# A two-block transformer on one core: gates' forget row after the second decay, 29 slabs split ahead, a later spread of the latents' norms, two merging products interleaved

## The chip, the core and the metric

One of the cores of a Trainium2 chip runs the whole program: TensorE (PE, matmuls), VectorE (DVE), ScalarE (ACT), GpSimd (POOL) and SyncE (SP), whose queue issues nearly all DMAs. The metric is the device time of one execution in microseconds. The kernel before takes 1064.96 us (median of three runs, 1063.67 to 1065.72).

## What is computed

One sequence of 512 tokens, width 1024, in fp32, through two blocks. The reference, cut to its lines of substance:

```python
# block 1: three mixers, then an MLP
h = rmsnorm(x, ln1); z = h @ w_in          # u_pool, gq, gk, gv, gg, ga, fq, fk, fv, ff
log_a = log_sigmoid(ga @ w_a_up + b_a) / 16        # GLA: per-channel decay, cumulated in chunks of 64
o = (q*exp(b-ref) . k*exp(ref-b), causal) v + (q*exp(b)) S_prev      # GLA output, per-head norm, silu gate
F = cumsum(log_sigmoid(ff + b_f))                  # FoX: forget row of 8 heads
p = softmax(q k^T / 8 + F_t - F_s)                 # FoX attention
x = x + concat(pool, gla, fox) @ w_o
x = x + (silu(gate) * up) @ w_down                 # gate, up = rmsnorm(x, ln2) @ w_gu, width 2816
x = rmsnorm(x, ln_f)
# block 2: MLA and DSA side by side
q_lat, c_kv, k_rope, z_a, q_b, k_b, v_b, z_b, q_idx, k_idx, w_idx, gate_a, gate_b = rmsnorm(x) @ w_in_2
q = rmsnorm(q_lat) @ w_uq; k, v = rmsnorm(c_kv) @ w_ukv; q_pe, k_pe = rope(...)
y_a = chunk-causal softmax attention (8 heads) * silu(z_a)
score = sum_h relu(q_idx . k_idx) * w_idx;  top-128 keys per query
y_b = softmax attention on those keys with a relative bias (8 heads) * silu(z_b)
merged = sigmoid(gate_a) * (y_a @ w_o_a) + sigmoid(gate_b) * (y_b @ w_o_b)
out = rmsnorm(x + merged @ w_out)
```

## The kernel before

**Products.** An fp32 operand is split into two parts that TensorE takes at full rate, hi (L188, an ACT copy) and lo (L190, source minus hi, on DVE or POOL). A product is three matmuls per 128-row slice: hi x hi, hi x lo, lo x hi (`dense`, L207; all matmuls are recorded at L151, transposes at L158). A slab of weights is 128 x 1024 (512 KB): `weight` (L196) loads it raw (`wr`) and splits it into `wh` and `wl`, and every third or so of the lo parts goes to POOL. For block 2, 33 slabs are split during block 1's MLP: `store` (L247) loads `sr`, ACT makes `sh`, POOL makes `sl`, and two DMAs write them to DRAM (`h_...`, `l_...`). `ready` (L237) later loads both parts back, or, for a slab that is not stored, calls `weight`.

**Order.** PE's order is written by hand: generators yield delays in ns of a modelled clock (`QKW`, `RSW`, `LATR` and the like), and a loop runs whichever is due, filling with products. The other engines' instructions are ordered by a scheduler, each engine then runs its own in order, and each waits for the semaphores of what it reads. SP issues its DMAs in order too, so a load that waits for its buffer holds up all behind it.

**The places touched.** (1) The GLA stage has two chains, f = 0 and 1 (`chain`, L753). `gates` (L608) makes the low-rank gate `ga` and the forget logits of FoX, and from these at once the forget row `F` (log-sigmoid L458 to L467 on 8 x 512, a scan at L620). `decay` (L655) makes a chain's log-sigmoid on 128 x 512 and its scan L660; `state` (L687) transposes the scaled keys (`kt`, copied by ACT at L693) and multiplies them with the values (`sc<-gv`); `output` (L715) makes the masked intra-chunk scores (`at`, L722) and multiplies them with the values (`pv<-at`). (2) `mlp` (L887) runs in two halves of 11 gate/up pairs (`w1gu`) and then 8 down products (`w1d`, slabs `wd` of 128 x 1408, hi and lo `wdh` and `wdl`). `relative` (L868) writes a 2.6 MB table (`shear`) in the first half's down products. The list `ahead` names the slabs to store; one is stored behind each gate/up pair but the first, one behind each down product of half 0, one behind each odd one of half 1. (3) `rstd` (L314) of the two latents of MLA: column sums, 1/sqrt, two parts (L298, L299), then after `RSW` = 800 ns of modelled clock the spread over 128 rows by eight matmuls with an identity (`tr<-identr,part`). (4) `merge_b` (L1312): eight output slices m, each a product of the DSA output (`lat`, four slices of 128) with `w2ob`; m = 0 and 1 share one slab. Before it `merge_a` products (L1246, closing at L1252) use the same three banks `mm`.

Of the kernel before, what the change touches and what calls it, by code (L numbers as in the profile page):

```python
# [20 lines left out]
P = 128  # L21
# [12 lines left out]
XR = 7  # L34
XO = 4
RSW = 800
RRW = 3300
KTW = 800
ATW = 2400
# [3 lines left out]
QKW = 500  # L43
# [41 lines left out]
class Body:  # L85
# [225 lines left out]
        self.spreaded = getattr(last, "ins", last)  # L311
        return r

    def rstd(self, sums, n):  # L314
        with self.tc.high_priority():
            c = self.inv_sqrt(self.col_sum(sums)[0], n)
            parts = self.parts(c)
        yield RSW
        with self.tc.high_priority():
            return self.spread(parts), c  # L320

# [261 lines left out]
    def gla_phase(self, ctx, h, R, Rc, mix, mp, b, fd, psg, held, V, proj):  # L583
        nc, A = self.nc, self.A
        gp = self.pool(ctx, "gla")
        new = b
# [21 lines left out]
        def gates():  # L608

            z, t = new()[:64], self.tmp()[:64]  # L610
            nc.scalar.activation(t, psg[64:], AF.Copy)
            with self.tc.issue_after(self.parted):
                nc.vector.tensor_tensor(z, psg[:64], t, op=OP.add)
            nc.vector.tensor_tensor(ga, z[:16], R[:16], op=OP.mult)
            f = new()[:8]
            nc.vector.tensor_tensor(f, z[32:40], R[32:40], op=OP.mult)
            F = self.log_sigmoid(f, self.gain("b_f", 0, 8), 8, new)
            one = new()[:8]
            nc.gpsimd.memset(one, 1.0)
            nc.vector.tensor_tensor_scan(F, one, F, 0.0, op0=OP.mult, op1=OP.add)  # L620
            nc.sync.dma_start(fd, F)

# [32 lines left out]
        def decay(f, q, k):  # L655
            ps = self.bank("tr")
            self.mm(ps, wau[:, f * P:(f + 1) * P], ga)
            la = self.log_sigmoid(ps, self.gain("b_a", f), P, new)
            bc = new()
            nc.vector.tensor_tensor_scan(bc, rmask, la, 0.0, op0=OP.mult, op1=OP.add)  # L660
            b3 = c3(bc)
            r = {}

            def scaled(name, base, src, scale):
                e = new()
                nc.scalar.activation(e, src, AF.Exp, scale=scale)
                nc.vector.tensor_tensor(e, base, e, op=OP.mult)
                r[name] = e

            def minus(c):  # L670
                d = new()
                nc.vector.tensor_tensor(c3(d), b3, b3[:, :, c:c + 1].to_broadcast([P, 8, 64]), op=OP.subtract)
                return d

            d = minus(63)
            scaled("kl", k, d, -1 / 16)
            dec = gp.tile([P, 8], F32, tag="dec", name="dec", bufs=2)
            nc.scalar.activation(dec, b3[:, :, 63], AF.Exp, scale=1 / 16)
            nc.vector.memset(dec[:, 0:1], 0.0)
            r["dec"] = dec  # L680
            d = minus(31)
            scaled("qi", q, d, 1 / 16)
            scaled("ki", k, d, -1 / 16)
            scaled("qx", q, bc, 1 / 16)
            return r
# [67 lines left out]
        def chain(f, held=None):  # L753
            if f == 0:
                gates()
            q, k = yield from qk(f, held)
            yield QKW + 3000 * (held is not None)
            r = decay(f, q, k)
            yield DECW
            sb = yield from state(f, r)  # L760
            gs[f] = yield from gate(f)
            yield GOW
            yield from output(f, r, sb, gs[f])

        gs = {}

        def pooling(f):

# [118 lines left out]
    def mlp(self, ctx):  # L887
        nc, A, x = self.nc, self.A, self.x
# [28 lines left out]
        t2 = lambda name, a, b: [("w2s", T2[name] + i, 1024) for i in range(a, b)]  # L917
        ahead = [("w2m", 0, KD * 72)] + t2("c_kv", 0, 2) + t2("q_idx", 0, 2) + t2("q_lat", 0, 3) + [("w2kv_v", 0, 1024)]
        ahead += t2("gate_b", 0, 8) + [("w2uq_r", 0, 768), ("w2pair", 0, 640)]
        for p in range(4):  # L920
            ahead += t2("gate_a", 2 * p, 2 * p + 2 if p < 3 else 6) + t2("z_a", p, p + 1)
            ahead += [("w2pair", p + 1, 640)] if p < 3 else []
        ahead = deque(ahead)
        relative = self.relative(wd)
        turns = []
        for half in range(2):
# [15 lines left out]
                    self.store(wd, *ahead.popleft())  # L942
            for m in range(KD):
                ps = self.all(self.dense(down(m, half), act, kt=FH))
                if (m % 2 or half == 0) and ahead:
                    self.store(wd, *ahead.popleft())
                if half == 0 and m < 2:
                    next(relative)
# [40 lines left out]
    def block2(self, ctx, psm, psc):  # L989
# [88 lines left out]
        def latent(name, n, gname, ps=None):  # L1078
# [10 lines left out]
                self.square_into(ss, z, j == 0)  # L1089
                out.append((zh, zl))  # L1090
            yield LATR
            r, c = yield from self.rstd([ss], n * P)
            return out, r, c

        V, V2 = [[], []], [[], []]
# [211 lines left out]
        gf = [at("qf", 1), at("kf", 1)]  # L1307
        for c in range(2):
            nc.sync.dma_start(gf[c], A["gf"][:, c * 512:(c + 1) * 512].to_broadcast([P, 512]))
        mg, wb, wo = [], {}, {}  # L1310

        def merge_b(m):  # L1312
            ga, gb = self.sx(), at("z", 3)
            nc.sync.dma_start(ga, kept["ma", m])
            nc.sync.dma_start(gb, kept["gate_b", m])
            if m % 2 == 0:
                wb[0] = self.weight(A["w2ob"][m // 2])
            ps = self.all(self.dense(wb[0], yb, kt=4, w0=(m % 2) * 512))
            nc.vector.scalar_tensor_tensor(gb, gb, 1.0, ps, op0=OP.add, op1=OP.mult)
            nc.vector.tensor_tensor(ga, ga, gb, op=OP.add)  # L1320
            hi = at("V", 8, dt=F32R)
            lo = qk(F32R) if m < 6 else self.kst()
            self.split_scaled(hi, lo, ga, 0.5)
            mg.append((hi, lo))
# [205 lines left out]
```

## Time and profile before

| | |
|---|---|
| median of three runs | 1064.96 us |
| profiled execution | 1063.43 us, of which its span 1061.7 |
| PE busy | 1042.3 us, 98% of the span, 5264 matmuls |
| DVE, ACT, POOL busy | 644.2 (61%), 548.3 (52%), 371.1 (35%) |
| granted TensorE clock, mean | 0.996 of full speed |
| DMA | 177.38 MB, mean 167 GB/s |

The profile page gives these sums. What it does not give is where PE stands still: that is in the view of waits of PE, and in tables of windows, which show the granted clock beside the busy time of each engine.

### The profile page before, as it was taken

The numbers are of one execution on the slowest core, as the hardware profiler recorded it, in microseconds if no ns is written. First come the engines' busy times: TensorE is split into PE (matmuls) and PEld (weight loads), VectorE is DVE, ScalarE is ACT, GpSimd is POOL, SyncE is SP. The second block draws the span as 40 slices with busy tenths as digits, with TensorE's granted clock in tenths as the row PEclk, the third lists the DMA queues.
The fourth block names the chain that finished last, engine by engine and source line by source line (L and its number), as shares of the span: only waits on it lengthen the run. The fifth ranks groups of instructions, "written<-read, shape, count | busy, mean of one in ns | idle before, by whom it ended". The sixth has DMA issues, their size and how long they took to land.

```text
span 1061.7 us, 14307 instructions
## 1 busy us (share of the span) xinstructions
PE 1042.3 (98%) x5264; PEld 864.3 (81%) x5264; DVE 644.2 (61%) x1141; ACT 548.3 (52%) x956; POOL 371.1 (35%) x213
## 2 busy tenths in 40 slices
PE   9999999999999999999999999999999999999997
PEld 6788977788888877888888888888888898888786
DVE  7754488866554523445433435799995556787652
ACT  7763478746343322333325545645555657777233
POOL 1233331233464531445424410010003345655354
PEclk9999999999999999999999999999999999999999
DMA  6312122126667688876777244464553323435842
GB/s 228 105 60 80 41 100 90 59 78 219 217 229 252 231 276 312 291 241 206 242 260 254 97 139 159 154 219 160 178 183 120 111 78 120 129 99 162 279 146 80
DMA packets 60126, 177.38 MB, mean 167 GB/s; under 512 B 7000, under 2 KB 11496, under 8 KB 60056
## 3 DMA queue, kind: packets, MB, share of 16 engines
q1 hardware_dynamic: 56968, 170.15, 47.6%
q10 hardware_dynamic: 2448, 4.22, 1.0%
q0 software_dynamic: 640, 2.10, 0.5%
q8 instruction: 42, 0.69, 0.3%
q14 instruction: 28, 0.23, 0.1%
HBM read 134.66 MB, written 44.40 MB: 169 GB/s over the span
## 4 chain that ended last, share of the span: by engine, by line
PE 47%; DVE 10%; DMA 3%; ACT 2%; issue 1%; SPq 1%; POOL 1%; ACTq 0%; DVEq 0%; POOLq 0%
PE mm L151 39%; PE sc L151 3%; DVE score L1068 2%; PE pv L151 2%; PE tr L158 2%; DVE m L1067 2%; DMA wd<-in_w1d 2%; PE tr L151 1%; DVE kst L190 1%; SPq L251 1%; DVE s L400 1%; DVE z L1203 1%; DMA z<-gate_a 1%; DVE pl L418 1%; DVE score L1052 1%
## 5 line engine op out<-in xcount | busy, mean ns | idle before, releaser
L151 PE MATMUL mm<-hh,wh 128*128 128x512 f32 (+2 forms) x808 | 323.2, 400 | 0.1
L151 PE MATMUL mm<-hl,wh 128*128 128x512 f32 (+3 forms) x808 | 315.2, 390 | 0.6 <-DVE hl L526 0.5
L151 PE MATMUL mm<-hh,wl 128*128 128x512 f32 (+1 forms) x800 | 312.4, 391 | 0.0
L190 POOL TENSOR_TENSOR wl<-wr,wh 128x1024 fp32r<-128x1024 f32 x74 | 186.6, 2522 | 328.6 <-ACT wh L188 307.2
L188 ACT ACTIVATE wh<-wr 128x1024 fp32r<-128x1024 f32 (+1 forms) x110 | 115.1, 1046 | 175.3 <-PE mm L151 150.1
L151 PEld LDWEIGHTS mm<-hh,wh 128*128 128x128 f32 (+1 forms) x808 | 152.3, 189 | 30.8 <-issue 1.3
L151 PEld LDWEIGHTS mm<-hh,wl 128*128 128x128 f32 (+1 forms) x800 | 150.1, 188 | 32.1
L151 PEld LDWEIGHTS mm<-hl,wh 128*128 128x128 f32 (+2 forms) x808 | 151.8, 188 | 29.1 <-DVE hl L526 1.8
L190 POOL TENSOR_TENSOR sl<-sr,sh 128x1024 fp32r<-128x1024 f32 (+3 forms) x32 | 81.9, 2558 | 81.0 <-DMA l_w2s<-sl 52.0
L151 PE MATMUL mm<-fh,wdh 128*128 128x512 f32 x176 | 71.0, 404 | 1.6 <-ACT wdh L188 1.6
L151 PE MATMUL mm<-fh,wdl 128*128 128x512 f32 x176 | 70.3, 400 | 0.9 <-DVE wdl L190 0.9
L151 PE MATMUL mm<-fl,wdh 128*128 128x512 f32 x176 | 70.1, 398 | 0.0
L938 DVE TENSOR_TENSOR u<-mm,R 128x512 f32<-128x512 f32 x22 | 15.2, 691 | 67.2 <-PE mm L151 67.2
L418 DVE TENSOR_TENSOR pl<-tr,ph 128x128 fp32r<-128x128 f32 (+1 forms) x96 | 45.9, 483 | 13.2 <-ACT ph L417 12.2
L402 ACT ACTIVATE s<-s,m 128x128 f32<-128x128 f32 (+1 forms) x64 | 35.8, 560 | 32.0 <-DVE m L400 31.6
L190 DVE TENSOR_TENSOR fl<-u,fh 128x512 fp32r<-128x512 f32 x22 | 42.4, 1925 | 14.7 <-ACT fh L188 14.7
L188 ACT ACTIVATE sh<-sr 128x1024 fp32r<-128x1024 f32 (+3 forms) x32 | 31.7, 990 | 37.3 <-DMA h_w2s<-sh 30.2
L949 DVE TENSOR_TENSOR x<-mm,x 128x512 f32<-128x512 f32 x16 | 11.1, 691 | 65.0 <-PE mm L151 65.0
L190 DVE TENSOR_TENSOR wl<-wr,wh 128x1024 fp32r<-128x1024 f32 (+1 forms) x35 | 42.9, 1226 | 11.0 <-ACT wh L188 10.6
L329 POOL TENSOR_TENSOR ss<-ss,t 128x512 f32<-128x512 f32 x21 | 29.7, 1423 | 55.3 <-ACT t L328 43.5
L151 PE MATMUL mm<-wh,hh 128*128 128x256 f32 x160 | 46.6, 291 | 0.0
L417 ACT ACTIVATE ph<-tr 128x128 fp32r<-128x128 f32 (+1 forms) x96 | 40.4, 425 | 10.1 <-PE tr L158 9.4
(343 smaller groups left out, 2053.3 us busy)
## 6 DMA issues: line engine op xcount, KB each, us to landing
wr<-in_w1gu SPq DMA_DIRECT2D x44, 512.0 KB, 4.6
sr<-in_w2s SPq DMA_DIRECT2D x25, 512.0 KB, 5.0
h_w2s<-sh SPq DMA_DIRECT2D x25, 512.0 KB, 2.9
l_w2s<-sl SPq DMA_DIRECT2D x25, 512.0 KB, 3.4
wh<-h_w2s SPq DMA_DIRECT2D x25, 512.0 KB, 3.7
wl<-l_w2s SPq DMA_DIRECT2D x25, 512.0 KB, 4.6
wd<-in_w1d SPq DMA_DIRECT2D x16, 704.0 KB, 5.7
wr<-in_w1s SPq DMA_DIRECT2D x15, 512.0 KB, 3.5
```

The lines of the kernel that those rows point to most:

```text
L151: self.nc.tensor.matmul(out, l, r, start=start, stop=stop)
L158: self.nc.tensor.transpose(out, src, self.ident if ident is None else ident)
L188: last = self.nc.scalar.activation(hi, src, AF.Copy)
L190: (eng or self.nc.vector).tensor_tensor(lo, src, hi.bitcast(F32), op=OP.subtract)
L329: return (eng or nc.gpsimd).tensor_tensor(ssum, ssum, sq, op=OP.add)
L402: nc.scalar.activation(s[:, :n], s[:, :n], AF.Exp, scale=-1.0, bias=m[:, 0:1], accum_out=m[:, 1:2])
L417: nc.scalar.activation(hi, trv, AF.Copy)
L418: nc.vector.tensor_tensor(lo, trv, hi.bitcast(F32), op=OP.subtract)
L938: nc.vector.tensor_tensor(u, ps, self.R2, op=OP.mult)
L949: nc.vector.tensor_tensor(x[m], ps, x[m], op=OP.add)
L1067: nc.vector.max(out=m8, in_=s)
L1068: nc.vector.match_replace(s, m8, s, -3.4e38)
```

## The change

- `gates` only keeps the logits `f`; the log-sigmoid and scan of the forget row are a function `forget`, called inside the second decay, behind its product with `wau`. The chain f = 0 takes its decay after `QKW` + 1000 instead of + 3000 ns.
- The list `ahead` loses four slabs (pairs' slab 3, `z_a` 3, `gate_a` 4 and 5), and in half 0 of the MLP a slab is stored only behind odd down products. The four slabs are loaded raw and split where they are used.
- The latents' `rstd` waits `LSW` = 3000 instead of `RSW` = 800 ns before the spread.
- The first two products of `merge_b` are written by `first_two`: two banks, slices k = 0 to 2 of both, then k = 3 of both.

```diff
--- before.py
+++ after.py
@@ -34,6 +34,7 @@
 XR = 7
 XO = 4
 RSW = 800
+LSW = 3000
 RRW = 3300
 KTW = 800
 ATW = 2400
@@ -311,11 +312,11 @@
         self.spreaded = getattr(last, "ins", last)
         return r
 
-    def rstd(self, sums, n):
+    def rstd(self, sums, n, lag=RSW):
         with self.tc.high_priority():
             c = self.inv_sqrt(self.col_sum(sums)[0], n)
             parts = self.parts(c)
-        yield RSW
+        yield lag
         with self.tc.high_priority():
             return self.spread(parts), c
 
@@ -612,8 +613,11 @@
             with self.tc.issue_after(self.parted):
                 nc.vector.tensor_tensor(z, psg[:64], t, op=OP.add)
             nc.vector.tensor_tensor(ga, z[:16], R[:16], op=OP.mult)
-            f = new()[:8]
+            logits["f"] = f = new()[:8]
             nc.vector.tensor_tensor(f, z[32:40], R[32:40], op=OP.mult)
+
+        def forget():
+            f = logits["f"]
             F = self.log_sigmoid(f, self.gain("b_f", 0, 8), 8, new)
             one = new()[:8]
             nc.gpsimd.memset(one, 1.0)
@@ -655,6 +659,8 @@
         def decay(f, q, k):
             ps = self.bank("tr")
             self.mm(ps, wau[:, f * P:(f + 1) * P], ga)
+            if f == 1:
+                forget()
             la = self.log_sigmoid(ps, self.gain("b_a", f), P, new)
             bc = new()
             nc.vector.tensor_tensor_scan(bc, rmask, la, 0.0, op0=OP.mult, op1=OP.add)
@@ -754,7 +760,7 @@
             if f == 0:
                 gates()
             q, k = yield from qk(f, held)
-            yield QKW + 3000 * (held is not None)
+            yield QKW + 1000 * (held is not None)
             r = decay(f, q, k)
             yield DECW
             sb = yield from state(f, r)
@@ -762,7 +768,7 @@
             yield GOW
             yield from output(f, r, sb, gs[f])
 
-        gs = {}
+        gs, logits = {}, {}
 
         def pooling(f):
 
@@ -918,8 +924,8 @@
         ahead = [("w2m", 0, KD * 72)] + t2("c_kv", 0, 2) + t2("q_idx", 0, 2) + t2("q_lat", 0, 3) + [("w2kv_v", 0, 1024)]
         ahead += t2("gate_b", 0, 8) + [("w2uq_r", 0, 768), ("w2pair", 0, 640)]
         for p in range(4):
-            ahead += t2("gate_a", 2 * p, 2 * p + 2 if p < 3 else 6) + t2("z_a", p, p + 1)
-            ahead += [("w2pair", p + 1, 640)] if p < 3 else []
+            ahead += t2("gate_a", 2 * p, 2 * p + 2 if p < 2 else 4) + t2("z_a", p, min(p + 1, 3))
+            ahead += [("w2pair", p + 1, 640)] if p < 2 else []
         ahead = deque(ahead)
         relative = self.relative(wd)
         turns = []
@@ -942,7 +948,7 @@
                     self.store(wd, *ahead.popleft())
             for m in range(KD):
                 ps = self.all(self.dense(down(m, half), act, kt=FH))
-                if (m % 2 or half == 0) and ahead:
+                if m % 2 and ahead:
                     self.store(wd, *ahead.popleft())
                 if half == 0 and m < 2:
                     next(relative)
@@ -1089,7 +1095,7 @@
                 self.square_into(ss, z, j == 0)
                 out.append((zh, zl))
             yield LATR
-            r, c = yield from self.rstd([ss], n * P)
+            r, c = yield from self.rstd([ss], n * P, LSW)
             return out, r, c
 
         V, V2 = [[], []], [[], []]
@@ -1307,15 +1313,33 @@
         gf = [at("qf", 1), at("kf", 1)]
         for c in range(2):
             nc.sync.dma_start(gf[c], A["gf"][:, c * 512:(c + 1) * 512].to_broadcast([P, 512]))
-        mg, wb, wo = [], {}, {}
+        mg, wb, wo, head = [], {}, {}, []
+
+        def first_two():
+
+            wb[0] = self.weight(A["w2ob"][0])
+            out = [self.bank("mm") for _ in range(2)]
+            for ks in (range(3), range(3, 4)):
+                for m in range(2):
+                    for k in ks:
+                        (hi, lo), (ah, al), c = wb[0], yb[k], slice(m * 512 + k * P, m * 512 + (k + 1) * P)
+                        self.mm(out[m], hi[:, c], ah, k == 0, False)
+                        self.mm(out[m], hi[:, c], al, False, False)
+                        self.mm(out[m], lo[:, c], ah, False, k == 3)
+            return out
 
         def merge_b(m):
             ga, gb = self.sx(), at("z", 3)
             nc.sync.dma_start(ga, kept["ma", m])
             nc.sync.dma_start(gb, kept["gate_b", m])
-            if m % 2 == 0:
-                wb[0] = self.weight(A["w2ob"][m // 2])
-            ps = self.all(self.dense(wb[0], yb, kt=4, w0=(m % 2) * 512))
+            if m < 2:
+                if m == 0:
+                    head.extend(first_two())
+                ps = head[m]
+            else:
+                if m % 2 == 0:
+                    wb[0] = self.weight(A["w2ob"][m // 2])
+                ps = self.all(self.dense(wb[0], yb, kt=4, w0=(m % 2) * 512))
             nc.vector.scalar_tensor_tensor(gb, gb, 1.0, ps, op0=OP.add, op1=OP.mult)
             nc.vector.tensor_tensor(ga, ga, gb, op=OP.add)
             hi = at("V", 8, dt=F32R)
```

The number of matmuls is the same, and so are the instructions of DVE, ACT and POOL in number and kind; SP issues 358 DMAs instead of 374. Lines below L311 have a number one or more higher after the change.

**ACT in the GLA stage**, from the scaling of chain 0's keys to the end of chain 1's log-sigmoid (`wh<-wr` is the hi part of a weight slab, `b<-tr` at L693 the copy of the transposed keys, L705 and L712 chain 0's state, L462 to L464 a log-sigmoid). Before:

```order
L666 ACTIVATE b<-b 128x512 x3
L188 ACTIVATE wh<-wr 128x1024 x2
L693 ACTIVATE b<-tr 128x512
L705 ACTIVATE b<-sc 64x256 x4
L712 ACTIVATE ph<-b 64x7x64 x2
L188 ACTIVATE wh<-wr 128x1024
L462 ACTIVATE b<-tr,gains 128x512
L463 ACTIVATE b<-b 128x512
L464 ACT_TABLE_LOAD
L464 ACTIVATE b<-b 128x512
```

After, from that copy (L699) on; two `wh<-wr` stand right ahead of the first row:

```order
L699 ACTIVATE b<-tr 128x512
L189 ACTIVATE wh<-wr 128x1024
L711 ACTIVATE b<-sc 64x256 x4
L463 ACTIVATE b<-b,gains 8x512
L718 ACTIVATE ph<-b 64x7x64 x2
L464 ACTIVATE b<-b 8x512
L465 ACT_TABLE_LOAD
L465 ACTIVATE b<-b 8x512
L189 ACTIVATE wh<-wr 128x1024
L463 ACTIVATE b<-tr,gains 128x512
L464 ACT_TABLE_LOAD
L464 ACTIVATE b<-b 128x512
```

The copy of the keys now stands ahead of the third slab instead of behind both; the forget row's log-sigmoid (8x512), which stood at the stage's start, now lies between chain 0's state and chain 1's log-sigmoid. That one ends two rows below the second fence (a table load and L465 on 128x512), so that three table loads stand there where one stood. On PE the four transposes of the keys and the eight `sc<-gv` products behind them stand nine 128x512 matmuls earlier, and chain 1's product with `wau` 18 128x256 matmuls earlier in its stage.

**SP in the down products of half 0**, from the shear table on (`sr` loads a slab to be stored, `h_` and `l_` write its parts, `wd` loads a down slab). Before:

```order
L884 DMA shear<-gd 1024x1x640
L251 DMA sr<-in_w2s 128x1024
L258 DMA h_w2s_3619<-sh 128x1024
L258 DMA l_w2s_3621<-sl 128x1024
L251 DMA sr<-in_w2s 128x1024
L900 DMA wd<-in_w1d 128x1408 x2
L258 DMA h_w2s_3670<-sh 128x1024
L258 DMA l_w2s_3672<-sl 128x1024
L251 DMA sr<-in_w2s 128x1024
L900 DMA wd<-in_w1d 128x1408
```

After:

```order
L890 DMA shear<-gd 1024x1x640
L252 DMA sr<-in_w2s 128x1024
L906 DMA wd<-in_w1d 128x1408
L259 DMA h_w2s_3742<-sh 128x1024
L906 DMA wd<-in_w1d 128x1408
L259 DMA l_w2s_3744<-sl 128x1024
L252 DMA sr<-in_w2s 128x1024
L906 DMA wd<-in_w1d 128x1408
L259 DMA h_w2s_3834<-sh 128x1024
L906 DMA wd<-in_w1d 128x1408
```

The first `wd` stood fifth behind the shear table and now stands second; between two `wd` there are now one or two of the stores' DMAs instead of three.

**PE in the first products of `merge_b`**; `lat` are the four slices of the DSA output, the one with the highest number the last to be made. Before (the end of the first product, the start of the second):

```order
L151 MATMUL mm_9244<-lat_8994,wh_9240 128x512
L151 MATMUL mm_9244<-lat_8995,wh_9240 128x512
L151 MATMUL mm_9244<-lat_8994,wl_9241 128x512
L151 MATMUL mm_9244<-lat_9207,wh_9240 128x512
L151 MATMUL mm_9244<-lat_9208,wh_9240 128x512
L151 MATMUL mm_9244<-lat_9207,wl_9241 128x512
L151 MATMUL mm_9267<-lat_8339,wh_9240 128x512
L151 MATMUL mm_9267<-lat_8340,wh_9240 128x512
L151 MATMUL mm_9267<-lat_8339,wl_9241 128x512
L151 MATMUL mm_9267<-lat_8676,wh_9240 128x512
L151 MATMUL mm_9267<-lat_8677,wh_9240 128x512
L151 MATMUL mm_9267<-lat_8676,wl_9241 128x512
```

After (the second bank's three slices, then the last slice in the first bank):

```order
L152 MATMUL mm_9213<-lat_8307,wh_9208 128x512
L152 MATMUL mm_9213<-lat_8308,wh_9208 128x512
L152 MATMUL mm_9213<-lat_8307,wl_9209 128x512
L152 MATMUL mm_9213<-lat_8644,wh_9208 128x512
L152 MATMUL mm_9213<-lat_8645,wh_9208 128x512
L152 MATMUL mm_9213<-lat_8644,wl_9209 128x512
L152 MATMUL mm_9213<-lat_8962,wh_9208 128x512
L152 MATMUL mm_9213<-lat_8963,wh_9208 128x512
L152 MATMUL mm_9213<-lat_8962,wl_9209 128x512
L152 MATMUL mm_9212<-lat_9175,wh_9208 128x512
L152 MATMUL mm_9212<-lat_9176,wh_9208 128x512
L152 MATMUL mm_9212<-lat_9175,wl_9209 128x512
```

Nine matmuls of the second product have moved ahead of the first one that reads the last slice.

## Rows read from the trace of the kernel before

**Rows 1.** Waits of PE: line, waited for, us in total, times, longest.
```profile
PE sc L151 <- ACT b L693: 1.8, 1, 1.8
PE mm L151 <- DVE lat L190: 1.6, 1, 1.6
PE mm L151 <- ACT wdh L188: 1.6, 1, 1.6
...
PE tr L151 <- DVE part L298: 1.1, 2, 0.9
PE mm L151 <- DVE wdl L190: 0.9, 1, 0.9
...
PE tr L151 <- DVE part L299: 0.5, 1, 0.5
```

**Rows 2.** Windows: length, busy PE, PEld, DVE, ACT, POOL, PEclk, DMA share, GB/s.
```profile
48.00:54.00 6.00, 6.00 (x29) 4.97 (x30) 1.81 (x2) 3.53 (x6) 0.00 (x0) 0.72 0.27 89
418.00:422.00 4.00, 4.00 (x12) 3.10 (x11) 2.52 (x1) 1.45 (x2) 2.37 (x1) 0.57 0.93 297
```

**Rows 3.** Timeline, GLA stage, ACT: start, duration, operation, [idle before, releaser].
```profile
29.18 1.28 ACT L464 ACT_TABLE_LOAD   x1
...
46.27 1.06 ACT L188 ACTIVATE wh<-wr 128x1024 fp32r<-128x1024 f32 x1 [3.87 <-DMA wr<-in_w1s]
47.23 0.58 ACT L693 ACTIVATE b<-tr 128x512 f32<-128x512 f32 x1
49.05 1.62 ACT L705 ACTIVATE b<-sc 64x256 f32<-64x256 f32 x4 [1.25 <-PE sc L151]
...
55.85 0.69 ACT L462 ACTIVATE b<-tr,gains 128x512 f32<-128x512 f32 x1 [0.61 <-PE tr L151]
...
58.52 0.63 ACT L464 ACTIVATE b<-b 128x512 f32<-128x512 f32 x1
```

**Rows 4.** Timeline, GLA stage, PE (two rows) and DVE (one).
```profile
47.86 1.72 PE L151 MATMUL sc<-gv,b 64*128 64x128 f32 x16 [1.83 <-ACT b L693]
...
71.33 1.58 PE L151 MATMUL pv<-at,gv 128*64 128x128 f32 x16
...
68.93 0.74 DVE L722 COPY_PREDICATED at<-c_gmask,sc 128x512 f32<-128x512 int32 x1
```

**Rows 5.** Timeline, down products of half 0: SP's queue, ACT, DVE; a window.
```profile
388.40 6.83 SPq L251 DMA_DIRECT2D sr<-in_w2s  x1
...
397.83 3.92 SPq L900 DMA_DIRECT2D wd<-in_w1d  x2
...
414.14 1.38 ACT L188 ACTIVATE wdh<-wd 128x1408 fp32r<-128x1408 f32 x1 [3.13 <-DMA wd<-in_w1d]
...
415.55 1.62 DVE L190 TENSOR_TENSOR wdl<-wd,wdh 128x1408 fp32r<-128x1408 f32 x1 [8.57 <-ACT wdh L188]
...
396.00:400.00 4.00, 4.00 (x18) 3.21 (x18) 0.92 (x2) 1.39 (x1) 0.00 (x0) 1.00 0.89 294
```

**Rows 6.** Latents and MLA: DVE's rope splits, then two windows as in rows 2.
```profile
667.10 2.08 DVE L190 TENSOR_TENSOR qk<-y,qk 32x512 fp32r<-32x512 f32 x2 [0.42 <-ACT qk L188]
...
680.00:700.00 20.00, 20.00 (x90) 16.47 (x89) 17.22 (x29) 11.54 (x21) 4.78 (x3) 1.00 0.59 203
740.00:760.00 20.00, 20.00 (x104) 16.93 (x103) 19.70 (x55) 11.43 (x25) 1.47 (x1) 1.00 0.58 197
```

**Rows 7.** Timeline: a DVE split in MLA; then the merge, DVE, POOL, PE.
```profile
791.51 0.68 DVE L190 TENSOR_TENSOR ya<-y,ya 128x512 fp32r<-128x512 f32 x1
...
988.17 2.08 DVE L190 TENSOR_TENSOR lat<-y,lat 128x512 fp32r<-128x512 f32 x1 [0.70 <-ACT lat L188]
992.01 0.69 DVE L1252 SCALAR_TENSOR_TENSOR z<-z,mm 128x512 f32<-128x512 f32 x1 [1.77 <-DMA z<-gate_a]
...
987.24 2.46 POOL L190 TENSOR_TENSOR wl<-wr,wh 128x1024 fp32r<-128x1024 f32 x1 [0.36 <-ACT wh L188]
...
993.66 0.62 PE L151 MATMUL mm<-lat,wh 128*128 128x512 f32 x2
```

## The prediction

> **What bounds the kernel now.** I read the view of PE's waits first. PE is busy for nearly the whole span, so only what makes it stand still, or run at half clock, can change the time. The waits that the four parts of the change aim at are in [rows 1]: 1.83 us for the copied keys of GLA (ACT b, L693), 1.6 + 0.9 for the hi and lo of one down slab, 1.1 + 0.5 for the parts of the latents' norms, 1.6 for the last slice of the DSA output; together 7.5 us. [...] The timeline is third: it says for each place what would be late next.
>
> **Part 1, the gates.** PE waited until 47.86 for ACT's copy of the transposed keys, and that copy, 0.58 us at 47.23, lay behind a weight split that ACT began at 46.27 after 3.87 us of waiting for the slab's DMA [rows 3, 4]. In the new order the copy is ahead of that split, and the transposes come nine matmuls earlier. The wait and the slow clock behind it go: 1.83 + 1.7 = 3.5 us.
> What is late next is chain 1's decay. On ACT its log-sigmoid ended at 58.52 + 0.63 = 59.15 [rows 3]; ahead of it now lie the forget row's three operations, taken at 0.63 each by the row of L464 since eight rows are as wide (1.9 us), and two more table loads at 1.28 (2.6 us): 4.5 us. One of the three can run while ACT waits for chain 0's scan, and the 0.61 us that ACT stood idle at 55.85 [rows 3] go too; 3.2 us remain. Against that the part begins earlier: the first copies of chain 0's state (L705) stood at 49.05. Now the third slab's split stands right ahead of them; if its DMA comes as late as before they begin at 46.27 + 1.06 = 47.33, 1.7 us earlier, and if the DMA is earlier they follow `sc<-gv`, which comes 1.83 + 2.1 (nine matmuls) earlier, less some 0.8 for the rest of the split in front: up to 3.1 us earlier. So the log-sigmoid ends 0.1 to 1.5 us later than before, while PE is 3.5 us ahead. From it an unbroken chain of DVE operations leads to the masked scores (L722), which ended at 68.93 + 0.74 = 69.67; PE used them at 71.33, a slack of 1.66 [rows 4]. PE will come to them at 71.33 - 3.5 = 67.8 and find them at 69.8 to 71.2: a new wait of 2.0 to 3.4 us, `pv<-at` on DVE `at`. Part 1 is worth 0.1 to 1.5 us; I take 1.0. If the clock falls after the new wait as it did after the old one, a further 1.7 are lost, and the lower bound is -1.6.
>
> **Part 2, the down slab.** The slab that PE waited for was issued on SP at 397.83, behind a store's load that the queue could not issue from 388.40 to 395.23, and behind two writes and one more load of the stores [rows 5]. ACT had it only at 414.14 [rows 5], so it took 16 us from issue to landing, with the DMA engines full. The new queue issues it right behind the blocked load. That is 397.83 - 395.23 = 2.6 us earlier, and three transfers of 512 KB (1.57 MB) no longer precede it: at the 294 GB/s of that window [rows 5] they took 5.3 us. So it lands 2.6 to 5.3 us earlier, at 408.8 to 411.5. To keep PE busy, the hi part (1.38 us on ACT) and the lo part (1.62 us on DVE) must be ready in time. PE first stopped at 414.14 + 1.38 - 1.6 = 413.9, and between its two waits it worked from 415.5 to 415.55 + 1.62 - 0.9 = 416.3, 0.8 us on hi alone [rows 1, 5]; so hi is needed at 413.9 and lo at 414.7, which is 3.0 us after a landing by 411.7. Both bounds meet it, the weaker one just. I take the whole of 1.6 + 0.9 + 1.7 = 4.2 us, with 0 as the other end if the queue's block moves along with the slab.
> The four slabs no longer stored save four loads and eight writes in the MLP, where nothing waited for them, and cost a split each where they are used; that is in part 3.
>
> **Part 3, the latents' norms and the slabs split at use.** The spread stands some nine matmuls (2 us) later on PE, longer than any of the three waits for the parts: 1.6 us go. The rows R that depend on it come 2 us later, and with them the rope of the shared keys on DVE, whose last two splits alone took 2.08 us [rows 6]. In 680 to 700 DVE has 2.8 us idle, in 740 to 760 only 0.3 [rows 6]; what is not absorbed by 700 is carried through the MLA stage to PE, which has next to no slack there. That costs 0 to 2.1 us; I take 0.5, since the idle time is larger than the work that moves.
> The four slabs add four POOL splits of up to 2.46 us (the row of the same shape in [rows 7]). A DVE split of 128x512 takes 0.68 alone and took 2.08 beside such a POOL split [rows 7]: it ended at 990.25, 0.55 us after POOL, so it had waited for it. [...] The ACT halves (1.06 us each, the row of that form in [rows 3]) go into ACT's idle time, 20 - 11.43 us of 20 in [rows 6]. Part 3: 1.6 - 0.5 - 1.0 = +0.1 us.
> [...]
>
> **Part 4, the merge.** PE waited 1.6 us for the lo part of the last slice, which was ready at 988.17 + 2.08 = 990.25 [rows 1, 7]. From 990.25 to the start of the third product at 993.66 lie two matmuls of the first and twelve of the second, so one takes 3.4 / 14 = 0.24 us [rows 7]; nine of the second product (2.1 us) now fill that time. Without the wait the third product would begin at 992.0, but it needs the bank that L1252 reads from 992.01 to 992.70, which waits for a DMA of a gate and not for PE [rows 7]. So it begins at 992.75: 0.9 us are gained, not 1.6. Bounds 0.4 (the gate lands later) and 1.6.
>
> **Sum.** 1.0 + 4.2 + 0.1 + 0.9 = 6.2 us. The profiled execution took 1063.43 (span 1061.7), so 1057.2; it lies 1.5 below the median of the runs, so the forecast for the median is 1058.8.
>
> **The rivals.**
> A. All four waits go and nothing takes their place: 10.9 us, 1054.1. For it: each wait's direct cause is moved away. Against it: the slack of 1.66 at `pv<-at` and the gate's DMA at 992 stand in the trace.
> B. The gates give all back: the new wait is 3.4 us and the clock falls again, part 1 is -1.6 instead of 1.0: gain 3.6, 1061.4. For it: 1.83 us of standstill were followed by such a fall; against it: 1.6 us at the merge were not, [rows 2] lists both slow stretches.
> C. The change doesn't do what it says in the MLP: the load in front still blocks and the slab lands as late as before. Gain 6.2 - 4.2 = 2.0, 1063.0.
> D. Slower than before: POOL's splits at use hold up DVE in the MLA stage, where DVE is busy 19.7 of 20 us and PE follows it. Each of the four then costs its whole 2.46, 9.8 instead of 1.0: 1058.8 + 8.8 = 1067.6. It makes the kernel slower once a slab costs more than (6.2 + 1.0) / 4 = 1.8 us. [...]
>
> **How the numbers follow.** About 0.2% (2.1 us) is what a measurement of this kernel can tell from no change. Forecast 0.52, A 0.14, B 0.16, C 0.10, D 0.08. Predicted 1058.8. Faster than 1062.8: forecast, A and B, 0.82. C lies within 0.2%, and half of D with a smaller price: 0.14. Slower: 0.04, the rest of D. The range reaches below A's 1054.1 by little and above B's 1061.4 by the bounds of part 4 and of the rope, 1053.5 to 1062.6; left out are D, most of C and the lower edge of A, under 0.2.
>
> **What would show it.** Right: the wait `sc<-gv` on ACT b is gone from PE's waits and a wait of `pv` on DVE `at` of 2 to 3.4 us is there; no waits on `wdh` or `wdl`, and clock 1.00 around 410 to 422; no waits on `part`; in the merge no wait on `lat`, but one of about 1 us on L1252's bank. MLA: a few tenths to 2 us of new waits on DVE. Wrong would be: a slow clock behind `pv<-at` (B), a wait for `wdh` near 408 to 414 (C), or long waits in the MLA stage behind DVE operations that ended with a POOL split (D).

## The result

The changed kernel took 1057.47 us in the median of four runs (1055.76 to 1059.30) where the kernel before took 1064.32 beside it; the ratio is 0.9937, 95% interval 0.9916 to 0.9959. Measured again (ten runs, `after_again` below) it was 0.9945, 0.9928 to 0.9961: 4 to 8 us faster. The forecast was 1058.8.

The profiled execution of the changed kernel took 1059.30 us, the slowest of the first four, with a span of 1057.4 against 1061.7 before. So its trace explains 4.3 us; the rest is in what one execution doesn't show, and the experiments come to that. It is the slowest of the four though its mean granted clock, 0.999, is the highest. The waits of PE in it (line, waited for, us in total, times, longest), to be read against [rows 1]:

```profile
PE tr L159 <- ACT s L408: 2.3, 1, 2.3
...
PE mm L152 <- DVE z L1258: 1.5, 1, 1.5
...
PE tr L159 <- DVE s L406: 1.1, 2, 0.6
PE mm L152 <- ACT wdh L189: 0.9, 1, 0.9
PE mm L152 <- DVE wdl L191: 0.9, 1, 0.9
PE mm L152 <- DVE V L444: 0.9, 1, 0.9
...
PE pv L152 <- DVE at L728: 0.3, 1, 0.3
```

Gone are the waits for the copied keys, for the norms' parts and for the last slice of the DSA output. The down slab still costs 0.9 + 0.9 instead of 1.6 + 0.9. New are the masked scores (0.3), the values V (0.9), an exponential of the MLA attention (2.3, ACT s L408) and the merge's bank (1.5, L1258). The clock no longer falls in the two stretches of [rows 2]:

```profile
48.00:54.00 6.00, 6.00 (x25) 4.12 (x24) 1.57 (x4) 5.44 (x6) 0.00 (x0) 1.00 0.22 83
418.00:422.00 4.00, 4.00 (x19) 3.23 (x18) 0.36 (x1) 0.60 (x1) 1.26 (x1) 1.00 0.89 278
```

PEclk, the column behind the five engines, is 1.00 in both, where it was 0.72 and 0.57. All waits in the view add up to some 12.5 us, as many as before: in this trace most of the gain is the 3.4 us that the two falls had cost. In the second trace of the change the waits add up to some 10 us, and the mean granted clock is 0.997, which at 1057 us is some 2 us of work less.

**A ledger.** The plainest way to see what each part gave is to take one matmul behind each place and compare its start in the two traces. Before and after, from the timeline of PE:

```profile
54.70 1.12 PE L151 MATMUL tr<-ga,c_wau 16*128 16x512 f32 x2
72.84 1.38 PE L151 MATMUL sc<-gv,b 64*128 64x128 f32 x13
421.41 0.43 PE L151 MATMUL mm<-fl,wdh 128*128 128x512 f32 x1
685.00 0.63 PE L151 MATMUL mm<-lat,wh 128*128 128x512 f32 x2
794.23 0.55 PE L158 MATMUL tr<-c_ident,s 128*128 128x128 f32 x3 [0.20 <-ACT s L407]
...
801.51 0.66 PE L158 MATMUL tr<-c_ident,s 128*128 128x128 f32 x4
962.42 0.30 PE L158 MATMUL tr<-c_ident,s 128*128 128x128 f32 x1
```

```profile
51.33 1.12 PE L152 MATMUL tr<-ga,c_wau 16*128 16x512 f32 x2
70.35 1.71 PE L152 MATMUL sc<-gv,b 64*128 64x128 f32 x16
416.77 0.40 PE L152 MATMUL mm<-fl,wdh 128*128 128x512 f32 x1
679.23 0.63 PE L152 MATMUL mm<-lat,wh 128*128 128x512 f32 x2
787.26 0.54 PE L159 MATMUL tr<-c_ident,s 128*128 128x128 f32 x3
...
796.96 0.66 PE L159 MATMUL tr<-c_ident,s 128*128 128x128 f32 x4 [2.28 <-ACT s L408]
958.50 0.30 PE L159 MATMUL tr<-c_ident,s 128*128 128x128 f32 x1 [0.57 <-DVE s L406]
...
989.37 0.73 PE L152 MATMUL mm<-lat,wh 128*128 128x512 f32 x2 [1.48 <-DVE z L1258]
```

PE's lead is 54.70 - 51.33 = 3.4 us behind the gates, 2.5 at the end of GLA, 4.6 behind the down slab, 5.8 behind the latents, 794.23 - 787.26 = 7.0 just ahead of the stall of 2.28 us and 4.5 behind it, 3.9 behind one of 0.57, and 993.66 [rows 7] - 989.37 = 4.3 at the third merging product, where the span's 4.3 is reached. So part 1 kept 2.5, part 2 gave 2.1, part 3 gave 1.2 at the latents and 1.2 more in the MLA stage, where the stall took 2.4 again, and part 4 gave 0.4. A further 0.6 went at 958. The same wait of nearly 0.6 stands in the second trace of the change and in part 1 alone, and in these three traces alone a POOL addition near 951 took 1.18 or 1.19 us, where it takes 0.73 or 0.74 in all others, and the DVE split that began beside it 0.92 or 0.94, where it takes 0.69:

```profile
951.01 1.19 POOL L1286 TENSOR_TENSOR qk<-qk,score 128x256 f32<-128x256 f32 x1
...
950.67 0.92 DVE L349 TENSOR_TENSOR klo<-kf,kst 64x512 fp32r<-64x512 f32 x1
```

In these three DVE also stood idle for 0.35 us ahead of the operation before that split. Why it did is open.

### The profile page after: what moved, and what is told of

Read it like the earlier page. It is cut to its first block, busy times and chain, and to the rows that moved or that the text cites. A ratio compares the mean times of both kernels' runs of the same rounds, so it can differ in the third digit from the quotient of the medians.

```text
span 1057.4 us, 14279 instructions
## 1 busy us (share of the span) xinstructions
PE 1038.4 (98%) x5264; PEld 862.3 (82%) x5264; DVE 641.7 (61%) x1141; ACT 548.1 (52%) x956; POOL 371.2 (35%) x213
## 4 chain that ended last, share of the span: by engine, by line
PE 54%; DMA 4%; ACT 2%; DVE 2%; issue 1%; SPq 1%; POOL 1%; DVEq 0%; POOLq 0%; ACTq 0%
PE mm L152 45%; PE sc L152 4%; PE pv L152 2%; PE tr L159 2%; DMA wd<-in_w1d 1%; PE tr L152 1%; DMA ma<-z 1%; SPq L252 1%; DMA l_w2s<-sl 1%; POOL sl L191 1%; DMA z<-gate_a 0%; DMA wl<-l_w2s 0%; DVE kst L191 0%; DVE qst L343 0%; ACT s L403 0%
## 5 line engine op out<-in xcount | busy, mean ns | idle before, releaser
L191 POOL TENSOR_TENSOR wl<-wr,wh 128x1024 fp32r<-128x1024 f32 (+1 forms) x78 | 195.2, 2504 | 362.6 <-ACT wh L189 340.0
L189 ACT ACTIVATE wh<-wr 128x1024 fp32r<-128x1024 f32 (+2 forms) x114 | 118.8, 1043 | 174.4 <-PE mm L152 145.9
L191 POOL TENSOR_TENSOR sl<-sr,sh 128x1024 fp32r<-128x1024 f32 (+3 forms) x28 | 73.3, 2617 | 72.3 <-ACT sh L189 46.0
L189 ACT ACTIVATE wdh<-wd 128x1408 fp32r<-128x1408 f32 x16 | 22.1, 1380 | 62.4 <-PE mm L152 41.1
```

Of the source, the lines that this page charges most:

```text
L189: last = self.nc.scalar.activation(hi, src, AF.Copy)
L191: (eng or self.nc.vector).tensor_tensor(lo, src, hi.bitcast(F32), op=OP.subtract)
```

## The experiments

Times are medians, each beside runs of the kernel before on the same chip; the ratio is of this to the kernel before, with its 95% interval.

| kernel | us | before | ratio |
|---|---|---|---|
| part 1 alone | 1064.02 | 1063.07 | 1.0006 (0.9993 to 1.0019) |
| part 2 alone | 1064.23 | 1063.07 | 1.0002 (0.9983 to 1.0022) |
| part 3 alone, without its slabs at use | 1061.19 | 1063.07 | 0.9983 (0.9969 to 0.9997) |
| part 4 alone | 1063.22 | 1063.07 | 0.9999 (0.9981 to 1.0016) |
| the change, again | 1057.57 | 1064.00 | 0.9945 (0.9928 to 0.9961) |
| the change, 33 slabs stored | 1054.04 | 1064.00 | 0.9910 (0.9886 to 0.9934) |
| the change, shear table early | 1062.76 | 1064.00 | 0.9993 (0.9977 to 1.0008) |
| both of these | 1060.58 | 1064.00 | 0.9971 (0.9957 to 0.9986) |
| the new place of the stores alone, 33 slabs | 1058.89 | 1063.78 | 0.9959 (0.9943 to 0.9976) |
| that and part 1 | 1057.64 | 1063.78 | 0.9956 (0.9943 to 0.9970) |
| the change without part 1 | 1059.07 | 1063.78 | 0.9954 (0.9929 to 0.9978) |

### The four parts alone

Each is the kernel before with one part of the diff. The four ratios together make about 0.1%; the change is worth 0.55 to 0.63%. The traces say why.

**Part 1.**

> The kernel before with part 1 alone (forget row behind the second decay, chain 0's decay 2000 ns earlier in the modelled clock). Theory M (a DMA keeps its own time, so a wait for it grows by what PE gained upstream): the gates give 2.5 us (1.83 + 1.7, less some 0.9 of a new wait for the masked scores), but the down slab near 414 lands when it did, so PE's waits for its hi and lo parts grow from 2.5 to about 5 us; the whole kernel is 0 to 0.5 us faster. Rival A (the parts add up): the waits for the slab stay 2.5 us and the kernel is 2.5 us faster (ratio 0.9977).

Nothing in the time, as theory M had it. In the trace the gates give 2.3 us, and the down slab's waits are 2.3 + 0.9 instead of 1.6 + 0.9:

```profile
PE mm L151 <- ACT wdh L188: 2.3, 1, 2.3
...
PE mm L151 <- DVE wdl L190: 0.9, 1, 0.9
```

They grew by 0.7, not by the 2.5 that M named: the slab landed 1.5 us sooner than in the trace of before. But this profiled execution (1060.84) is the fastest of the twelve, and its clock did not fall behind the stall (1.00 from 414 to 422); the median is 3.2 us longer. Its mean granted clock is 0.998, that of the other eleven 0.993 to 0.996, which at 1060 us is 2 to 5 us of work less. So the others lost it to the clock; that they lost it at this place is likely and not shown.

**Part 2.** The diff is that of the list `ahead` and of the stores in half 0.

> The kernel before with part 2 alone (29 slabs, in half 0 one behind each odd down product). Theory M: the slab lands near 411.0 as in the changed kernel, and PE, not being 2.5 us ahead here, needs it at 411.7: no wait over 0.3 us at the slab and no fall of the clock there, 3.9 to 4.2 us gained at that place; behind it the four slabs split at use take back 0 to 2.5 in the MLA stage. In all 1.5 to 4.2 us faster. Rival A (the place is worth what the changed kernel shows): waits of 0.9 + 0.9 stay, 2.2 us gained there, in all 0 to 2.2.

At its place M holds in full: ACT began the slab's hi part at 409.65 instead of 414.14, PE waited for neither part, and its lead there grows by 4.6 us. Then the MLA stage takes 4.4 back, which is more than the price expected. Waits, then the window behind the stall, then GpSimd and VectorE at it (part 2 alone):

```profile
PE tr L158 <- ACT s L407: 2.8, 2, 2.6
```

```profile
799.00:803.00 4.00, 3.98 (x14) 3.41 (x15) 2.86 (x6) 2.29 (x5) 2.38 (x1) 0.57 0.01 2
```

```profile
792.68 2.40 POOL L190 TENSOR_TENSOR wl<-wr,wh 128x1024 fp32r<-128x1024 f32 x1 [3.07 <-ACT wh L188]
795.05 1.72 POOL L190 TENSOR_TENSOR qk<-kf,qk 64x512 fp32r<-64x512 f32 x1
...
793.12 2.51 DVE L190 TENSOR_TENSOR kst<-qf,qst 64x512 fp32r<-64x512 f32 x1
795.66 1.65 DVE L190 TENSOR_TENSOR kst<-qk,qst 32x512 fp32r<-32x512 f32 x1
...
798.05 0.15 DVE L403 RECIPROCAL m<-m 128x1 f32<-128x1 f32 x1
```

A slab's lo part is on POOL until 795.08; the DVE split that began beside it ends at 795.63, 0.55 us later, and the next one ends 0.54 behind the next POOL operation. Between them they take 4.16 us where the same two took 1.36 in the trace of before. The reciprocal that PE's transposes wait for stands behind them. The stall of 2.6 us is followed by a granted clock of 0.57 for 4 us, (1 - 0.57) x 4 = 1.7 us of work less.

**Part 3.** `LSW` alone, with all 33 slabs stored as before.

> The kernel before with part 3 alone (3000 instead of 800 ns before the spread of the latents' norms; the 33 slabs stay stored). Theory M: the waits for the parts (1.6 us) go, some 0.9 us of a new wait for the values (V) comes, and since no slab is split at use there is no stall of 2 us behind GpSimd's splits near 800: 0.7 to 1.6 us faster. Rival A (the later rope on VectorE is carried through the MLA stage, not the splits at use): a stall of about 2 us near 800 is here too, and the kernel is 0 to 1 us slower.

Faster by 1.9 us in the median, and the stall near 800 is 0.7 and not 2 us:

```profile
PE mm L152 <- DVE V L444: 0.9, 1, 0.9
...
PE tr L159 <- ACT s L408: 0.7, 1, 0.7
```

Rival A falls: the stall of 2 us belongs to the slabs split at use. Nor is the 0.7 shown to be a price of the later rope: counted from the latents on, PE comes to that place 1.2 us sooner than before and then waits 0.7. This profiled execution (1065.53) is the slowest of the thirteen, so its waits are read here and not its length.

**Part 4.** The interleaved products alone.

> The kernel before with part 4 alone (the first two merging products interleaved). The wait of 1.6 us for the last slice goes, a wait of about 1 us for the bank that L1252 reads takes its place: 0.4 to 0.9 us faster, which five rounds can hardly tell from nothing; the trace decides. Rival A: no new wait, 1.6 us faster.

```profile
PE mm L151 <- DVE z L1252: 0.8, 1, 0.8
```

The wait for the last slice is gone and one of 0.8 for the bank is there, so about 0.8 us remain, which the interval in the table can't tell from nothing.

### The change again, with 33 slabs, and with an early shear table

> The changed kernel once more, as the yardstick of this call. Theory M: the same waits at the same places as in its first trace (about 0.9 + 0.9 for the down slab at 411, 2.3 near 795 behind GpSimd's split, 1.5 at the merge), since each is set by the program and by DMA times; whether the clock falls behind one of them differs from run to run and makes the spread of some 3 us. Ratio 0.992 to 0.996. Rival A (the first measurement was luck, as the parts alone summed to about nothing): ratio 0.998 to 1.000.

The ratio holds and rival A falls: the parts do not add. The stall of 2.3 us at the exponential is there again; the mean granted clock of this execution is 0.997, where it was 0.999 in the first trace. The down slab was ready 1 us sooner than in the first trace (hi part from 410.02 instead of 411.01), so PE waited 0.1 + 0.9 there and not 0.9 + 0.9. The ten runs lie between 1055.15 and 1059.82.

The next kernel stores all slabs again:

```diff
-            ahead += t2("gate_a", 2 * p, 2 * p + 2 if p < 2 else 4) + t2("z_a", p, min(p + 1, 3))
-            ahead += [("w2pair", p + 1, 640)] if p < 2 else []
+            ahead += t2("gate_a", 2 * p, 2 * p + 2 if p < 3 else 6) + t2("z_a", p, p + 1)
+            ahead += [("w2pair", p + 1, 640)] if p < 3 else []
...
-                if m % 2 and ahead:
+                if (m % 2 or half == 1) and ahead:
```

> The changed kernel, but with all 33 slabs stored: half 0 of the MLP stores behind odd down products only, half 1 behind every one. No slab is split at use any more. Theory M (GpSimd's split of a slab at use holds up VectorE near 795): the wait of 2.3 us there falls under 0.7, and the kernel is 2 to 4 us faster than the changed one, if the eight stores of half 1's down products do not make a down slab late there (that would show as a wait for wdh between 560 and 640). Rival A (the later rope or the values V make the stall): the wait of 2.3 us stays.

Its waits:

```profile
PE mm L152 <- DVE V L444: 0.9, 1, 0.9
PE tr L159 <- ACT s L408: 0.6, 1, 0.6
...
PE mm L152 <- DVE z L1258: 0.5, 1, 0.5
```

The stall is 0.65, nothing waits for a down slab in half 1, and the kernel takes 1054.04 us, 3.5 less than the change and 10 less than before. Against the first trace of the change its own gains 2.0 us at the down slab of half 0, which came at 409.2 and not 411.0, and 1.6 at the stall. It is the fastest one here: the gain of part 2 comes from where the stores stand, and storing four fewer only cost.

The next kernel moves the shear table:

```diff
                 if m == 0:
                     self.entry()
+                if m in (1, 2):
+                    next(relative)
...
-                if half == 0 and m < 2:
-                    next(relative)
```

> The changed kernel, but with the 2.6 MB shear table written behind the second and third gate/up pairs of half 0 instead of behind its first two down products. Theory M (the down slab is late because SP's queue stands behind the table's write and the DMA engines are full of it): the slab lands before 409 and both waits near 411 go, 1.9 us and now and then a fall of the clock: 1.9 to 3 us faster than the changed kernel, if the gate/up slabs near 270 keep ahead of PE. Rival A (the stores' own traffic makes it late): the waits stay at about 1.9.

M is right about the place: PE waits for no down slab. But the condition fails. In the new place the table stands ahead of the gate/up slabs, and one of them is late. SP's queue, the wait of PE and the window behind it:

```profile
269.54 0.76 SPq L890 DMA_DIRECT2D shear<-gd  x1
270.33 4.88 SPq L259 DMA_DIRECT2D h_w2m<-sh  x1
275.34 0.73 SPq L199 DMA_DIRECT2D wr<-in_w1gu  x1
```

```profile
PE mm L152 <- POOL wl L191: 3.7, 1, 3.7
```

```profile
293.00:300.00 7.00, 5.79 (x14) 4.53 (x15) 3.50 (x3) 2.06 (x4) 1.61 (x2) 0.52 0.80 281
```

The store's write behind the table held the queue for 4.88 us; in the down products the load behind it held it for 7.19 in the first trace of the change. The stall is 4 us with the one just ahead of it, and the clock behind it is 0.52 of full speed for 7 us, (1 - 0.52) x 7 = 3.4 us of work lost. In either place PE waited for the slab that was due behind the table: 0.9 + 0.9 us in the down products of the change, 4 here.

> The two edits before together on the changed kernel: the shear table early, and all 33 slabs stored with eight stores in half 1. Theory M: both gains, 4 to 6 us faster than the changed kernel, 1051 to 1053 where the kernel before takes 1063 to 1064; what is left is the merge's 1.5 us and the waits that all kernels share. Rival A: no more than the better one of the two, since a later wait (wdh in half 1, or the MLA stage) takes the rest.

Rival A, in another way than it says: the late gate/up slab takes more than the second edit gives, and 1060.58 is worse than 33 slabs without the move.

### Part 2 without its price, and part 1 on top

The first kernel is the kernel before with one line changed, the condition of the stores, `m % 2 or half == 1` instead of `m % 2 or half == 0`; the second has part 1 besides; the third is the change without part 1.

> The kernel before with only the place of the stores changed: all 33 slabs stored, in half 0 behind odd down products only, in half 1 behind every one. Theory G (part 2 alone came out at nothing because the splits at use took back at 796 what the down slab gave at 414): the waits for the slab go and no wait of 2 us comes near 796, so 2.5 us of waits and mostly 1.7 of clock are gained: 3 to 4.5 us faster, ratio 0.9960 to 0.9972. Rival L (it came out at nothing because clock falls at other places replace the one at 418): ratio 0.999 to 1.001.

4.6 us in its trace between 400 and 425 and none lost near 796, 4.9 in the median. Theory G holds: part 2 alone came out at nothing because the splits at use took it back.

> Part 1 and the stores of the run before together (no splits at use, no later spread, no interleaved merge). Theory G: part 1's 2.3 us are now kept, since the down slab lands some 3.5 us sooner after the table than before; the slab waits 0 to 1.9 us and the clock falls at neither place: 5 to 7 us faster, ratio 0.9934 to 0.9953. Rival L: part 1 was worth nothing alone because other waits draw clock falls, and it adds nothing here: ratio 0.996 to 0.998.

In the trace the lead over the kernel without part 1 is 3.5 us ahead of the down products (0.6 of it from ahead of the gates), 2.6 behind the slab and 2.0 at the end. The slab's waits are 0.7 in all, against 3.3 in part 1 alone.

The time is less clear. 1057.64 is 1.3 us under the kernel without part 1, but the two ratios differ by 0.0003 only, and 0.9956 lies between what G and what L named. Part 1 on top is worth 0 to 2 us, and neither theory is shown.

> The changed kernel without part 1 (forget row and decays as before). Theory G (a DMA's landing follows the queue more than PE): the 1.8 us for the copied keys are back, with or without a fall of the clock, but PE comes later to the down slab and waits for neither part; stall near 796 as in the changed kernel: 0.5 to 2.5 us slower than the changed kernel, ratio 0.995 to 0.997. Rival A (parts add): 2.5 to 3.5 us slower, ratio 0.997 to 0.998.

The slab's waits are gone as expected, and the wait of 1.8 us for the copied keys is back; the mean granted clock of this execution is 0.993, where it was 0.999 in the first trace of the change. The first trace of the change leads this one by 4.1 us ahead of the slab and by 1.7 behind it: the rest of what part 1 gave was lost there. The median is 1.5 us above the 1057.57 of the change, which was measured beside other runs of the kernel before; by the two ratios it is 1 us. The interval does not exclude the rival.

## Why the prediction was right, and where it was not

The median lies 1.3 us under the forecast and well inside the range. The sum was 6.2 us; the two measurements give 6 to 7. The terms hold less well, and that they sum to nearly the forecast is in part luck: part 1 gave 1.5 us more than taken, part 2 2.1 less, and the profiled execution, forecast at 1057.2, took 1059.30.

- **Part 1, "a new wait of 2.0 to 3.4 us".** Under-rated: the wait is 0.3, and 3.4 - 2.5 = 0.9 us of lead are lost there, since the sixteen `pv<-at` products, which took 1.58 us before [rows 4], now take 69.34 + 1.09 - 67.94 = 2.49. Two steps failed. The third slab's DMA was early, the case that I put at "up to 3.1 us" (the copies of chain 0's state came 49.05 - 45.51 = 3.5 earlier), so that the log-sigmoid ended at 58.78, 0.37 sooner than before and not 0.1 to 1.5 later. And the slack of 1.66 was read at the first of the sixteen `pv<-at` products. They run head by head: the first eight read only the first masked block, and only the second eight need the last one. In the trace of before the second eight ran partly beside the first, from 71.82 on, 0.5 us later; now they wait.

```profile
44.55 1.06 ACT L189 ACTIVATE wh<-wr 128x1024 fp32r<-128x1024 f32 x1 [1.20 <-DMA wr<-in_w1s]
45.51 1.63 ACT L711 ACTIVATE b<-sc 64x256 f32<-64x256 f32 x4
...
58.15 0.63 ACT L465 ACTIVATE b<-b 128x512 f32<-128x512 f32 x1
...
67.94 1.09 PE L152 MATMUL pv<-at,gv 128*64 128x128 f32 x8
69.34 1.09 PE L152 MATMUL pv<-at,gv 128*64 128x128 f32 x8 [0.30 <-DVE at L728]
```

The split at 44.55 stood at 46.27 in [rows 3]. One sentence ahead of the prediction needs a correction too: the `wau` product that moved 18 matmuls forward is the first decay's, chain 0's, and not chain 1's.

- **Part 2, "a landing by 411.7".** The landing was forecast rightly, 408.8 to 411.5; measured are 411.0 and 410.0 in the two traces of the change, 409.2 with 33 slabs and 409.7 in part 2 alone. What failed is the deadline. I took it from the trace of before, but PE comes 2.5 us sooner when part 1 has worked, so the deadline is 411.7 - 2.5 = 409.2. Of 4.2 us, 2.1 came, and 1.7 of these are the fall of the clock, which did not come although 1.9 us of waits stayed. Part 2 alone, where the deadline is the old one, gave all of it.

```profile
395.26 0.74 SPq L906 DMA_DIRECT2D wd<-in_w1d  x1
...
411.01 1.38 ACT L189 ACTIVATE wdh<-wd 128x1408 fp32r<-128x1408 f32 x1 [12.77 <-DMA wd<-in_w1d]
```

- **Part 3, "+0.1".** Right in sum (a lead of 4.6 behind the slab, 4.5 behind the stall), with the weights misplaced. The latents give 5.8 - 4.6 = 1.2 and not 1.6, since 0.9 of a wait for V takes the place of the 0.9 for the last of the parts [rows 1]. For the later rope, taken at -0.5, no trace shows a price: with part 3, in the change as alone, PE gained 1.2 us more in the MLA stage. No run shows the 1.0 taken for the splits at use; by the trace with 33 slabs they cost 2.28 - 0.65 = 1.6 us, all of it at one place:

```profile
790.98 2.40 POOL L191 TENSOR_TENSOR wl<-wr,wh 128x1024 fp32r<-128x1024 f32 x1 [3.17 <-ACT wh L189]
793.34 1.73 POOL L191 TENSOR_TENSOR qk<-kf,qk 64x512 fp32r<-64x512 f32 x1
...
791.62 2.30 DVE L191 TENSOR_TENSOR kst<-qf,qst 64x512 fp32r<-64x512 f32 x1
793.96 1.66 DVE L191 TENSOR_TENSOR kst<-qk,qst 32x512 fp32r<-32x512 f32 x1
```

This is what rival D named, at one of four slabs. The added POOL split also pushes the POOL operation behind it over the second DVE split: one slab stood in the way twice. In all four rows the times agree with a wait: the DVE splits end 0.54 and 0.55 us behind the POOL operations that they met (793.92 against 793.38, 795.62 against 795.07), and took 0.68 each in the trace of before (798.40 and 799.11). Not every DVE operation was held: `qf<-mm,R` at 786.61, which reads the bank `mm`, and MATCH_REPLACE8 at 787.27 took 0.67 us each inside the POOL split of 785.41 to 787.82.

- **Part 4, "0.9".** Right in kind: the third product waits for L1258. It gave 0.4, since the gate's DMA let L1258 begin 988.62 - 984.13 = 4.5 us after its issue, against 3.9 before; that is the bound named for it. In the second trace of the change the wait was 0.1, in part 4 alone 0.8.

- **The clock.** The falls at 48 and 418 went as forecast. The two terms of 1.7 us for them are (1 - 0.72) x 6 and (1 - 0.57) x 4 by [rows 2]; both windows show 1.00 after the change. In the first of them, before, the granted clock is 0.50 from 50 to 52 and the 128x512 matmuls on split parts start 0.43 us apart; at 1.00, from 53 to 54, they start 0.23 apart, and the product of `ga` with `wau`, which isn't split and has as many columns, takes 54.70 to 55.75, 1.05 us. What the forecast had for the gates only, in B, is that some stalls are followed by a fall and others are not, so that the same stall can be worth more in the median than in one trace. The mean granted clock is recorded for every execution. On average it is 0.9952 for the kernel before, 0.9975 for the ten later runs of the change and 0.999 for those with 33 slabs. (0.9975 - 0.9952) x 1060 = 2.4 us, so some 2.4 of the change's 6 to 7 us are clock. Parts 1 and 2 alone, at 0.9953 and 0.9956, gained nothing there. Followed by a fall were 1.83 us at the gates (0.72 for 6 us) and 1.6 + 0.9 at the down slab (0.57 for 4) in the trace of before, 2.6 at the exponential in part 2 alone (0.57 for 4), 3.6 + 0.4 at the down slab in part 4 alone (0.57 from 417 to 425, a stretch that holds a part of the stall) and 3.7 at the gate/up slab with the early table (0.52 for 7). Not followed by one were 2.3 + 0.9 at the down slab in part 1 alone (1.00 from 414 to 422), 0.9 + 0.9 there and 2.28 at the exponential in the first trace of the change (1.00 from 414 to 422 and from 797 to 799), and 1.6 at the merge before (1.00 from 990 to 994). Each of the falls at 0.57 for 4 us is 1.7 us of work, that at 0.52 for 7 is 3.4. A part of the parts' sum may have gone here, by my estimate: a stall that an edit left was followed by a fall in some traces.

Rival C did not come, nor B: behind `pv<-at` the granted clock stayed at 1.00 (66 to 72). A was ruled out by the slab's deadline, the V wait, POOL and the bank.

## What to carry to other kernels

When several waits in a row are removed, work each deadline out anew with what the places ahead of it give: the down slab kept its queue's pace, so its deadline came sooner by the 2.5 us that PE had gained, and the gains of such edits need not add. Work moved off a table of stored results did not go, here, where idle time is on the average but beside one operation on a busy engine; look for such operations by their times in the trace of before: there the DVE split `fl<-u,fh`, with both operands in SBUF, took 2.11 to 2.13 us the nineteen times that it began beside a POOL operation and 0.69 the three times that it did not, while `x<-mm,x`, which reads a bank, took 0.69 at 390.89, inside a POOL split of 390.47 to 392.88. And time an edit alone and in company: alone, three of these four edits measured as nothing.

## What the runs showed that I had not expected

- The stall behind a POOL split recurred: 2.3 us in each of the four traces with the change's order (2.28 in the first), 2.6 in part 2 alone. The down slab's hi part began between 408.7 and 411.3 in the seven traces with the stores in their new place and the table in its old one.
- Behind the 2.6 MB write of the table the next load or store on the same queue took 4.91 to 7.19 us to issue in the down products (part 3 alone, the first trace of the change) and 4.88 in the early place; the load behind that one took 0.73 there.
- A scan over 8 x 512 took 3.25 us on VectorE (54.47, the forget row behind the second decay), where it took 1.21 before and the 128 x 512 scans take 1.22. It began beside a POOL split that ended at 56.65 and ended 1.07 us behind it, as if it had waited too; it ran ahead of chain 1's log-sigmoid on DVE and was not in my sum.

```profile
54.26 2.39 POOL L191 TENSOR_TENSOR wl<-wr,wh 128x1024 fp32r<-128x1024 f32 x1 [10.77 <-ACT wh L189]
...
54.47 3.25 DVE L624 TENSOR_TENSOR_SCAN b<-b 8x512 f32<-8x512 f32 x1
...
59.54 1.22 DVE L666 TENSOR_TENSOR_SCAN b<-c_rmask,b 128x512 f32<-128x512 f32 x1
```
